# A hybrid decoder layer: an eighth Strassen pair in the up-projection, and the last gate's first half summed beside the out-projection

## The chip, the cores and the metric

The kernel runs on one core of a Trainium2 chip. Time is device microseconds of one launch, taken as the median of several executions. The core has a matrix engine (TensorE, PE in the profile, with its weight loads as PEld), a vector engine (DVE), an activation engine (ACT), a general engine (POOL) and a queue processor (SP). SP, ACT and POOL issue DMAs; each engine works through its own instructions in order.

## The reference

One layer for 512 tokens of width 1024. The condition `c` gives six rows of 1024 (shift, scale and gate of the two halves of the layer). The part that matters here is the second half, and the row `gt2`:

```python
mod = silu(c) @ w_ada + b_ada
sh1, sc1, gt1, sh2, sc2, gt2 = split(mod, 6)
...
x = x + gt1 * (concat(o_hg, o_nsa) @ w_out)
h2 = rmsnorm(x, norm2_g) * (1.0 + sc2) + sh2
u = causal_dwconv(h2 @ w_up, conv_w, conv_b)      # w_up: 1024 x 5632, width-3 convolution over tokens
a, v = split(u, 2)
x = x + gt2 * ((silu(a) * v) @ w_down)            # w_down: 2816 x 1024
```

All of it is float32. Every operand of a large matmul is held as two parts, high and low, and a product is three matmuls (high by high, high by low, low by high).

## The kernel before

**Order.** The instructions are issued in the order of the program, engine by engine; nothing reorders them. Tiles come from pools. The pool of granules (`G`, 33 of 4 KB in each partition) holds the long-lived parts; `TMP` gives temporaries, `PS` one of eight banks of PSUM.

**Tiles of the up-projection.** `up_mm(st)` makes tile `st` of 44: 128 rows of u by 512 tokens, 8 blocks of K by three matmuls, 24 matmuls of 512 columns. Tile `st` belongs to f = st // 2 (22 pairs of rows of a and v); even `st` is a, odd `st` is v. `up_post(st)` does the convolution (an activation on ACT, L1633, and two operations on DVE, L1634 and L1635), silu for a (L1638), and for v the product of the two (L1641); then `g_parts` queues the splits that the down-projection needs, and `step(n)` does n of these.

**Units.** Of four tiles, a unit makes the first two together by Strassen's scheme: seven products (P1 to P7) of half of K by half of the tokens, 12 matmuls of 256 columns each, in place of 48 of 512. The other two (B and C) are full tiles. The units are j = `NB` to `NU`; the string `UNIT` is their order, with a prime on a token that prepares the next unit. `PRO` is the order of the prologue that comes ahead: M1 to M7 are tiles 1 to 7 of the matmuls, q0 to q6 `up_post`, F and A the weight forms of a tile (`piece`), t the sums of h2 that the products need, x `step(1)`, n1', f2' and so on the forms of the first unit, m0' the weight forms of its first full tile. In an F form ACT makes the high part and DVE the low part; in an A form the low part is a negated copy by ACT to which POOL adds the source by an adding DMA (L260). After the units come plain tiles; `PLAIN` has a word for each, an A for an A form, and the number of gate steps.

**The gate.** `ada_last` makes `gt2` in two halves of 512 columns. Each half is zeroed, its first partition gets the bias, and eight blocks of rows of `w_ada` (256 KB each) are loaded, multiplied by a column of silu(c) and added, by DVE. The sum is split, and two matmuls with a matrix of ones (L1426, L1427) sum over the partitions and spread the row to all of them; ACT copies it back. It is a generator: the token g takes one step of it. Before, there are 20 steps: three g in `PRO`, one in each of the seven units, ten in the plain tiles, and all its loads are on SP's queue.

**The out-projection** runs ahead of that, tokens in four tiles: `hg_mix` and `hg_flip` make the left operand, `out_mm` the product, `out_sum` adds gate and residual, `out_norm` takes the norm, where `rstd` ends with a power on POOL (L393), `out_scale` and `h2_flip` turn the result.

**Parking.** The parts of a pair j of the down-projection are two granules, gP and gQ. For j in `AWAY`, gQ goes to memory (`park`, on ACT's queue) and comes back in the down-projection's first phase (`load_away`, called by `each_a` at every second step from the fourth on, on SP's queue).

Of the kernel before, what the change touches and what calls it, by code (L numbers as in the profile page):

```python
# [10 lines left out]
F32 = mybir.dt.float32  # L11
# [5 lines left out]
ALU = mybir.AluOpType  # L17
# [3 lines left out]
P = 128  # L21
# [17 lines left out]
SCRATCH = 1024  # L39
LAG = 4  # L40
NB = 2
NU = 8
AWAY = (0, 1)
CUT = {"B": 6, "C": 7}
ADD = (1, 1)
PLAIN = "2 A1 1 1 A2 1 1 1"
PRO = ("t t g x M1 M2 t t t t F3 M3 F4 t A5 q0 M4 q1 q2 F6 q3 M5 M6 A7 x q4 g x q5 x t x n1' ns' f2' nc' n5' q6 na' g s4' m0' x x M7 m1' x f6' f7' x x x x f4'")
UNIT = ("P1 S P5 w n1' ns' x f3 B0 P6 P2 B1 V x f2' nc' n5' h1 x p-1 f4' P7 x m0' P3 h0' W p2 g p0 na' C0 P4 x x x C1 s4' p1 x m1' x f6' x x x f7'")
PREP = ('sq2 sq3 rq2 rq3', '', 'nq0', 'fq0', 'nq1', '', 'lq0', 'fq1', 'nq2', '', 'lq1', 'fq2', 'nq3', 'lq2', 'fq3',
        'lq3', 'sk0 rk0 sk1 rk1', 'nk0 fk0 sk2 rk2', 'nk1 fk1 sk3 rk3', 'lk0 nk2 fk2', 'lk1 nk3 fk3 sa0 ra0',  # L50
# [61 lines left out]
def hybrid_layer_kernel(ctx: ExitStack, tc: tile.TileContext, d: dict, out: bass.AP, dbg=None):  # L112
# [24 lines left out]
    def TMP(shape, dt=F32, tag="tmp"):  # L137
        n = 1
        for a in shape[1:]:
            n *= a  # L140
        if n > 256:
            return tp.tile(shape, dt, tag="t2", name=nm(tag), bufs=9)
        return tp.tile(shape, dt, tag="t1", name=nm(tag), bufs=4)
# [4 lines left out]
    def f32(ap):  # L148
        return ap.bitcast(F32)

    def split(hi, lo, src, eng=None):
        sc.copy(hi, src)  # L152
        (eng or ve).tensor_tensor(lo, src, f32(hi), ALU.subtract)  # L153
# [236 lines left out]
    def rstd(o, s, scale, eps):  # L390
        n = s.shape[-1]
        ve.tensor_scalar(o, s, scale, eps, ALU.mult, ALU.add)  # L392
        gp.tensor_tensor(o, o, mhalf[:, 0:n], ALU.pow)  # L393
# [881 lines left out]
    ons = {}  # L1275
    mixH = [None] * NT

    def hg_mix(i):
        ps = PS("hgo")
        for h in range(4):  # L1280
            AD, QP, S = As[h // 2]
            j = h % 2
            pe.matmul(ps[:, h * P:(h + 1) * P], AD[:, j, i], HV[j][:, i, h // 2 * P:h // 2 * P + P], start=True,
                      stop=(i == 0))
            if i:
                pe.matmul(ps[:, h * P:(h + 1) * P], QP[:, j, i * P:(i + 1) * P], S[:, j, i - 1], start=False, stop=True)
        sq = TMP([P, 512], tag="sqh")
        sc.activation(sq, ps, AF.Square)
        s = SM([P, 8], "hss")
        ve.tensor_reduce(s[:, 0:4], sq.rearrange("p (h e) -> p h e", h=4), AX.X, ALU.add)  # L1290
        r = SM([P, 8], "hrs")
        rstd(r[:, 0:4], s[:, 0:4], 1.0 / P, 4.0 * EPS)
        on = TMP([P, 4, P], tag="on")
        ve.tensor_tensor(on, ps.rearrange("p (h e) -> p h e", h=4),
                         r[:, 0:4].unsqueeze(2).to_broadcast([P, 4, P]), ALU.mult)
        ons[i] = on

    def hg_flip(i):
        on = ons.pop(i)
        ps = PS()  # L1300
        for h in range(4):
            pe.transpose(ps[:, h * P:(h + 1) * P], on[:, h], ident)
        m = G([2, 4, P], F32R, s="mixH")
        t = TMP([P, 4, P], tag="og")
        for pr in range(2):
            ve.scalar_tensor_tensor(t[:, 2 * pr:2 * pr + 2], ps[:, pr * 256:pr * 256 + 256]
                                    .rearrange("p (h t) -> p h t", h=2), hgg,
                                    HGT[pr][:, :, i * P:(i + 1) * P], ALU.mult, ALU.mult)
        split(m[:, 0], m[:, 1], t)
        mixH[i] = m  # L1310


# [86 lines left out]
    def ada_last(s, res):  # L1399
        for q in range(2):  # L1400
            acc = res[:, q * 512:(q + 1) * 512]
            c0 = s * D + q * 512
            gp.memset(acc, 0.0)
            sp.dma_start(acc[0:1], d["b_ada"][:, c0:c0 + 512])
            for k in range(KT if q else 0):
                raw = TMP([P, 512], tag="ada2r")
                sp.dma_start(raw, ada_view[:, k, c0:c0 + 512])
                if k:
                    yield
                    ve.scalar_tensor_tensor(acc, last, cs[:, k - 1:k], acc, ALU.mult, ALU.add)  # L1410
                last = raw
            for k in range(0 if q else KT):
                last = res[:, 512:]
                if k:
                    ve.scalar_tensor_tensor(acc, last, cs[:, k - 1:k], acc, ALU.mult, ALU.add)
                sp.dma_start(last, ada_view[:, k, c0:c0 + 512])
                if k < KT - 1:
                    yield
            yield
            ve.scalar_tensor_tensor(acc, last, cs[:, k:k + 1], acc, ALU.mult, ALU.add)  # L1420
            hi = TMP([P, 512], F32R, tag="rhi")
            lo = TMP([P, 512], F32R, tag="rlo")
            split(hi, lo, acc)
            yield
            ps = PS()
            pe.matmul(ps, onesr, hi, start=True, stop=False)  # L1426
            pe.matmul(ps, onesr, lo, start=False, stop=True)  # L1427
            sc.copy(acc, ps)
            yield


    x1 = []
# [144 lines left out]
    for i in range(NT):  # L1577
        x1.append(G([D], s="x1"))
        sp.dma_start(x1[i], x_view[:, i])
    next(gate1)  # L1580
    hg_mix(0)
    next(gate1)
# [1 line left out]
    out_mm(0, 0, KN)  # L1584
    cols_sum(acol)
    hg_flip(0)
    hg_mix(2)
    hg_mix(3)
    out_mm(1, 0, KN)
    for _ in gate1:  # L1590
# [1 line left out]
    out_weights("oh", 0, 0)  # L1592
    out_mm(2, 0, KN)
    hg_flip(1)
    hg_flip(2)
    out_mm(3, 0, KN)
    out_mm(0, 0, KH)
    hg_flip(3)
# [146 lines left out]
    def do_(j, tok):  # L1745
        lo_, hi_ = lo_half, hi_half
        w = forms7.get(j)
        u = partial(u_of, j)
        if tok == "P1":
            banks(j)  # L1750
            sprod(u(1, lo_), w[1], h2_quarter(0, lo_), True)
        elif tok == "P5":
            sprod(us["x", j][:, lo_], w[5], h2_summed(1), True)
        elif tok == "P6":
            sprod(u(1, lo_), w[6], h2_summed(2))
        elif tok == "P2":
            sprod(u(0, lo_), w[2], h2_quarter(1, lo_))
        elif tok == "P7":
            sprod(u(1, lo_), w[7], h2_summed(3))
        elif tok == "P3":  # L1760
            sprod(u(0, hi_), w[3], h2_quarter(1, hi_))
        elif tok == "P4":
            sprod(u(1, lo_), w[4], h2_summed(4))
        elif tok in ("B0", "B1", "C0", "C1"):
            up_mm(4 * j + (2 if tok[0] == "B" else 3), full, (range(0, CUT[tok[0]]), range(CUT[tok[0]], KT))[int(tok[1])])
        elif tok == "S":
            sc.copy(u(0, lo_), u(1, lo_))
        elif tok == "w":
            spare(j)
        elif tok == "V":  # L1770
            ve.tensor_tensor(u(0, hi_), u(1, lo_), ws5[j], ALU.add)
        elif tok == "W":
            ve.tensor_tensor(u(1, hi_), u(1, lo_), ws5[j], ALU.add)
        elif tok[0] == "p":
            up_post(4 * j + int(tok[1:]))
        elif tok == "x":
            step(1)
        elif tok == "g":
            next(ada2, None)
        elif tok == "t":  # L1780
            turn()
        elif tok[0] == "m":
            std_make(j, int(tok[1]))
        elif tok[0] == "h":
            h = high.pop(4 * j + 2 + int(tok[1]))
            if h:
                h()
        elif tok == "n1":
            pair_open(j)
        elif tok == "ns":  # L1790
            pair_sum(j)
        elif tok == "nc":
            pair_less(j, 2, 0, 2)
        elif tok == "na":
            pair_less(j, 0, 4, 0)
        elif tok == "s4":
            pair_less(j, 1, 1, 0)
        elif tok == "n5":
            split(*w[5], quads[j][4])
        else:  # L1800
            pair_form(j, int(tok[1]), {6: 0, 2: 1, 7: 2, 3: 1, 4: 3}[int(tok[1])])
# [139 lines left out]
        ve.tensor_tensor(t, t, rest[i][:, cols], ALU.add)  # L1941
        sp.dma_start(out_view[:, i, cols], t)

    gt2 = wp.tile([P, D], F32, tag="xin", name="gt2", bufs=1)
    ada2 = ada_last(5, gt2)
    lo_half, hi_half, full = slice(0, 256), slice(256, 512), slice(0, 512)
    nst = 2 * NFF
    for i in range(NT):
        out_mm(i, 1, KN + KH)
        if i == 0:  # L1950
            conv_weights()
        if i:
            h2_flip(i - 1)
            wts[i - 1] = next_parts(False)
        out_sum(i, 1)
        sc.dma_start(x1d[:, i], x1[i])
        out_norm(i)
        if i:
            h2_scale(i - 1, 0)
            h2_scale(i - 1, 1)  # L1960
        out_scale(i)
        if i:
            h2_split(i - 1)
# [29 lines left out]
    for st in range(first, nst):  # L1993
        up_mm(st, full)
        if st >= nst - 2:
            look()
        if st == first:
            up_post(st - 1)
        elif st > first + 1:
            up_post(st - 2)  # L2000
        for _ in range(int(PLAIN.split()[st - first][-1])):
            next(ada2, None)

    look()
    up_post(nst - 2, False)
    bR, bW, bS, bV = ([PS("dn") for _ in range(2)] for _ in range(4))
# [101 lines left out]
```

## Time and profile before

| | us |
|---|---|
| median of 3 runs | 674.73 (674.34 to 675.54) |
| the profiled execution | 674.35 |
| its span, from the first to the last instruction | 672.6 |
| out-projection and its head, about | 267 to 326 |
| prologue of the up-projection | 326.9 to 372.3 |
| seven units | 372.3 to 520.2 |
| eight plain tiles | 520.2 to 564.2 |
| down-projection, first to last matmul | 564.2 to 669.1 |

A row of a timeline has start, length, engine, line of the program, operation, output <- inputs, shape and count; in brackets stands how long the engine was idle before it, and what ended that. A row of a group has the count, the busy time and the mean.

### The profile page before, as it was taken

To read this page: it belongs to the slowest core of one execution; us is meant where nothing else is said; L and a number is where in the kernel's file an instruction comes from. 1 tells how busy PE (TensorE), PEld (TensorE's weight loads), DVE (VectorE), ACT (ScalarE), POOL (GpSimd) and SP (SyncE) were. 2 spreads that over 40 slices of the span, in tenths; PEclk is the share of its full clock that TensorE was granted. 3 is DMA by queue.
4 is the path that set the end of the run, shared out by engine and by line. 5 is a ranking of instruction groups with operands and counts; after the bars stand their busy time and mean duration, and the time that the engine had idled before them with its cause. 6 is when DMAs were issued, how large, how long until landed. Compare 5 with 4: busy or idle time off the path is not lost.

```text
span 672.6 us, 10869 instructions
## 1 busy us (share of the span) xinstructions
PE 664.9 (99%) x3999; PEld 565.1 (84%) x3999; DVE 577.8 (86%) x1155; ACT 392.6 (58%) x757; POOL 60.0 (9%) x80
## 2 busy tenths in 40 slices
PE   8999999999999999999999999999999999999998
PEld 4678898788898889888998888989888888888886
DVE  5688988999998997687878988998898789988787
ACT  5564446666677688335665766667675455553431
POOL 1006144200000000200000011010110000000000
PEclk9999999999999999999999999999999999999999
DMA  9998444388042132435436677986779773979932
GB/s 279 287 322 269 145 157 138 106 288 254 11 147 95 33 107 99 172 96 161 140 95 172 179 196 198 242 218 175 187 181 277 217 234 124 393 259 398 388 112 94
DMA packets 110473, 128.52 MB, mean 191 GB/s; under 512 B 7067, under 2 KB 84691, under 8 KB 110421
## 3 DMA queue, kind: packets, MB, share of 16 engines
q1 hardware_dynamic: 103541, 106.89, 51.1%
q0 software_dynamic: 2448, 8.91, 6.9%
q10 hardware_dynamic: 4432, 12.04, 4.7%
q8 instruction: 31, 0.51, 0.3%
q14 instruction: 21, 0.17, 0.1%
HBM read 105.01 MB, written 13.90 MB: 177 GB/s over the span
## 4 chain that ended last, share of the span: by engine, by line
PE 92%; SPq 3%; DMA 2%; DVE 1%; issue 0%; ACTq 0%; ACT 0%
PE u L156 11%; PE u L158 11%; PE u L157 11%; PE dn L157 5%; PE dn L156 5%; PE dn L158 5%; PE pT L156 3%; PE pT L158 3%; PE pT L157 3%; PE F L1059 3%; PE oT L1087 3%; PE oh L158 2%; PE oh L156 2%; PE oh L157 2%; SPq L317 2%; PE lev L1188 2%
## 5 line engine op out<-in xcount | busy, mean ns | idle before, releaser
L156 PE MATMUL u<-h2h,whi 128*128 128x512 f32 (+1 forms) x208 | 78.0, 375 | 0.0
L157 PE MATMUL u<-h2l,whi 128*128 128x512 f32 (+1 forms) x208 | 77.8, 374 | 0.0
L158 PE MATMUL u<-h2h,wlo 128*128 128x512 f32 (+1 forms) x208 | 77.6, 373 | 0.0
L153 DVE TENSOR_TENSOR wlo<-raw,whi 128x1024 fp32r<-128x1024 f32 (+1 forms) x38 | 44.5, 1170 | 6.7 <-ACT whi L152 6.5
L152 ACT CAST whi<-raw 128x1024 fp32r<-128x1024 f32 (+1 forms) x38 | 38.3, 1008 | 18.8 <-PE u L157 7.3
L158 PEld LDWEIGHTS u<-h2h,wlo 128*128 128x128 f32 x208 | 39.2, 188 | 7.5 <-DVE wlo L153 0.4
L156 PEld LDWEIGHTS u<-h2h,whi 128*128 128x128 f32 x208 | 39.3, 189 | 6.0
L157 PEld LDWEIGHTS u<-h2l,whi 128*128 128x128 f32 x208 | 39.3, 189 | 5.8
L1027 ACT ACTIVATE pt<-pt,mx 128x128 f32<-128x128 f32 (+3 forms) x64 | 35.9, 562 | 11.8 <-DVE mx L1011 10.7
L1634 DVE SCALAR_TENSOR_TENSOR y<-u,cv,y 128x511 f32<-128x511 f32 x44 | 32.8, 745 | 11.4 <-ACT y L1633 11.4
L156 PE MATMUL pT<-hT,whi 128*128 128x512 f32 x96 | 39.2, 408 | 0.0
L1638 ACT ACTIVATE y<-y 128x512 f32<-128x512 f32 x21 | 13.3, 633 | 42.0 <-DVE y L1635 42.0
L158 PE MATMUL pT<-hT,wlo 128*128 128x512 f32 x96 | 37.7, 393 | 0.0
L157 PE MATMUL pT<-hT,whi 128*128 128x512 f32 x96 | 37.6, 391 | 0.0
L1011 DVE CUSTOM_DVE_ANT_0 pt<-S,cmask 128x128 f32<-128x128 f32 (+3 forms) x64 | 29.7, 484 | 6.5 <-PE S L1006 6.3
L1066 ACT COPY pT<-F 128x512 f32<-128x512 f32 (+2 forms) x52 | 25.9, 503 | 14.4 <-PE F L1059 11.2
L1635 DVE SCALAR_TENSOR_TENSOR y<-u,cv,y 128x510 f32<-128x510 f32 x44 | 32.9, 749 | 1.6
L1633 ACT ACTIVATE y<-u,cv 128x512 f32<-128x512 f32 x44 | 33.8, 771 | 0.0
L393 POOL TENSOR_TENSOR hrs<-hrs,mhalf 128x4 f32<-128x4 f32 (+2 forms) x16 | 20.0, 1259 | 136.4 <-DVE hrs L392 136.3
L157 PE MATMUL u<-h2l,w 128*128 128x256 f32 (+1 forms) x84 | 28.0, 333 | 0.0
L156 PE MATMUL u<-h2h,w 128*128 128x256 f32 (+1 forms) x84 | 28.0, 333 | 0.0
L158 PE MATMUL u<-h2h,w 128*128 128x256 f32 (+1 forms) x84 | 28.0, 333 | 0.0
(456 smaller groups left out, 2079.2 us busy)
## 6 DMA issues: line engine op xcount, KB each, us to landing
raw<-in_w_up SPq DMA_DIRECT2D x44, 512.0 KB, 5.6
aw<-in_w_ada SPq DMA_DIRECT2D x24, 512.0 KB, 3.6
raw<-in_w_down SPq DMA_DIRECT2D x10, 1024.0 KB
ada<-in_w_ada SPq DMA_DIRECT2D x32, 256.0 KB, 5.8
wlo<-raw POOLq DMA_DIRECT2D x15, 512.0 KB, 4.6
raw<-in_w_in SPq DMA_DIRECT2D x7, 1024.0 KB, 6.1
rawd<-in_w_down SPq DMA_DIRECT2D x12, 512.0 KB, 10.3
pk<-st ACTq DMA_DIRECT2D x11, 512.0 KB, 4.0
```

Of the source, the lines that this page charges most:

```text
L152: sc.copy(hi, src)
L153: (eng or ve).tensor_tensor(lo, src, f32(hi), ALU.subtract)
L156: pe.matmul(o, ah, bh, start=start, stop=False, skip_group_check=True)
L157: pe.matmul(o, ah, bl, start=False, stop=False, skip_group_check=True)
L158: pe.matmul(o, al, bh, start=False, stop=stop, skip_group_check=True)
L1011: ve.tensor_tensor_reduce(pt[:, sl], ps[:, sl], cmask[:, 512 - W:512], -1.0, 1e30, ALU.add, ALU.min, mx[:, e:e + 1])
L1027: sc.activation(pt[:, sl], pt[:, sl], AF.Exp, bias=mx[:, e:e + 1], scale=-1.0, accum_out=su[:, h % 2, e:e + 1])
L1059: pe.transpose(ps[:, j * P:(j + 1) * P], src[:, j * P:(j + 1) * P], ident)
L1066: sc.copy(pT, ps[:, 0:n * P])
L1633: sc.activation(y, u, AF.Identity, bias=cv[:, 132 + c:133 + c], scale=cv[:, 88 + c:89 + c])
L1634: ve.scalar_tensor_tensor(y[:, 1:], u[:, :T - 1], cv[:, 44 + c:45 + c], y[:, 1:], ALU.mult, ALU.add)
L1635: ve.scalar_tensor_tensor(y[:, 2:], u[:, :T - 2], cv[:, c:c + 1], y[:, 2:], ALU.mult, ALU.add)
```

## The change

`NU` goes from 8 to 9, so that the units are j = 2 to 9 and four plain tiles are left. `AWAY` goes from two granules to four. `ada_last` is cut into steps half as long (its load and its sum are separate steps, 40 in all), it takes its loads for the first half on POOL's queue and for the second on SP's, and each half has one buffer for its loads (the second half a stretch of the constants that is no longer read). It is made ahead of the out-projection: a first pair of steps there, one step within `hg_mix(2)` and one behind it, the same at `hg_flip(2)`, two in each of the four tiles of tokens around `out_norm`. Three g of two steps are in `PRO`, one in each unit, and one in each of the first two plain tiles.

```diff
-NU = 8
-AWAY = (0, 1)
+NU = 9
+AWAY = (0, 1, 2, 3)
-PLAIN = "2 A1 1 1 A2 1 1 1"
-PRO = ("t t g x M1 M2 t t t t F3 M3 F4 t A5 q0 M4 q1 q2 F6 q3 M5 M6 A7 x q4 g x q5 x t x n1' ns' f2' nc' n5' q6 na' g s4' m0' x x M7 m1' x f6' f7' x x x x f4'")
+PLAIN = "1 A1 0 A0"
+PRO = ("t t x M1 M2 t t t t F3 M3 F4 t A5 g q0 M4 g q1 q2 g F6 q3 M5 M6 A7 x q4 x q5 x t x n1' ns' f2' nc' n5' q6 na' s4' m0' x x M7 m1' x f6' f7' x x x x f4'")
...
-    def hg_mix(i):
+    def hg_mix(i, between=lambda: None):
...
         rstd(r[:, 0:4], s[:, 0:4], 1.0 / P, 4.0 * EPS)
+        between()
         on = TMP([P, 4, P], tag="on")
...
-    def hg_flip(i):
+    def hg_flip(i, between=lambda: None):
...
-        split(m[:, 0], m[:, 1], t)
+        sc.copy(m[:, 0], t)
+        between()
+        ve.tensor_tensor(m[:, 1], t, f32(m[:, 0]), ALU.subtract)
...
     def ada_last(s, res):
         for q in range(2):
             acc = res[:, q * 512:(q + 1) * 512]
+            last = cb[:, C_LMASK:C_LMASK + 512] if q else res[:, 512:]
             c0 = s * D + q * 512
             gp.memset(acc, 0.0)
-            sp.dma_start(acc[0:1], d["b_ada"][:, c0:c0 + 512])
...
+            gp.dma_start(acc[0:1], d["b_ada"][:, c0:c0 + 512])
+            for k in range(KT):
                 if k:
                     ve.scalar_tensor_tensor(acc, last, cs[:, k - 1:k], acc, ALU.mult, ALU.add)
...
+                yield
+                (sp if q else gp).dma_start(last, ada_view[:, k, c0:c0 + 512])
+                yield
             ve.scalar_tensor_tensor(acc, last, cs[:, k:k + 1], acc, ALU.mult, ALU.add)
             hi = TMP([P, 512], F32R, tag="rhi")
             lo = TMP([P, 512], F32R, tag="rlo")
             split(hi, lo, acc)
             yield
+            yield
             ps = PS()
             pe.matmul(ps, onesr, hi, start=True, stop=False)
             pe.matmul(ps, onesr, lo, start=False, stop=True)
             sc.copy(acc, ps)
             yield
+            yield
+
+    def gate_step(n=2):
+        for _ in range(n):
+            next(ada2, None)
...
+    gt2 = wp.tile([P, D], F32, tag="xin", name="gt2", bufs=1)
+    ada2 = ada_last(5, gt2)
+    gate_step()
     next(gate1)
...
-    hg_mix(2)
+    hg_mix(2, partial(gate_step, 1))
+    gate_step(1)
...
-    hg_flip(2)
+    hg_flip(2, partial(gate_step, 1))
+    gate_step(1)
...
         elif tok == "g":
-            next(ada2, None)
+            gate_step()
...
         sc.dma_start(x1d[:, i], x1[i])
+        gate_step(1)
         out_norm(i)
+        gate_step(1)
...
         for _ in range(int(PLAIN.split()[st - first][-1])):
-            next(ada2, None)
...
+            gate_step()
```

More of the change, by code (lines that the diff above doesn't have):

```diff
@@ L1401, in ada_last @@
             acc = res[:, q * 512:(q + 1) * 512]
+            last = cb[:, C_LMASK:C_LMASK + 512] if q else res[:, 512:]
             c0 = s * D + q * 512
             gp.memset(acc, 0.0)
-            sp.dma_start(acc[0:1], d["b_ada"][:, c0:c0 + 512])
[L1405 to L1413, printed above, removed]
+            gp.dma_start(acc[0:1], d["b_ada"][:, c0:c0 + 512])
+            for k in range(KT):
                 if k:
                     ve.scalar_tensor_tensor(acc, last, cs[:, k - 1:k], acc, ALU.mult, ALU.add)
[L1416 to L1419, printed above, removed]
+                yield
+                (sp if q else gp).dma_start(last, ada_view[:, k, c0:c0 + 512])
+                yield
             ve.scalar_tensor_tensor(acc, last, cs[:, k:k + 1], acc, ALU.mult, ALU.add)
@@ L1942, in dn_out @@
         sp.dma_start(out_view[:, i, cols], t)
-    gt2 = wp.tile([P, D], F32, tag="xin", name="gt2", bufs=1)
-    ada2 = ada_last(5, gt2)
     lo_half, hi_half, full = slice(0, 256), slice(256, 512), slice(0, 512)
@@ L2001, in hybrid_layer_kernel @@
         for _ in range(int(PLAIN.split()[st - first][-1])):
-            next(ada2, None)
+            gate_step()
+    assert next(ada2, 0) == 0
     look()
```

## The prediction, made before the changed kernel was run

> **What bounds the kernel now.** I read the page first: its span and its busy shares.
>
> ```profile
> span 672.6 us, 10869 instructions
> ...
> PE 664.9 (99%) x3999; PEld 565.1 (84%) x3999; DVE 577.8 (86%) x1155; ACT 392.6 (58%) x757; POOL 60.0 (9%) x80
> ```
>
> TensorE is busy for 664.9 of 672.6 us, so time can only come from fewer or shorter matmuls, or from new waits of TensorE. The table of who waited shows no idle TensorE after the first 100 us. A busy PE is modelled, though, so I read the spacing of matmul starts in the timeline of PE, over the whole up-projection.
>
> ```profile
> 361.44 0.39 PE L156 MATMUL u<-h2h,w 128*128 128x512 f32 x1
> ...
> 366.88 0.39 PE L156 MATMUL u<-h2h,whi 128*128 128x512 f32 x1
> ...
> 375.19 0.40 PE L156 MATMUL u<-h2h,whi 128*128 128x512 f32 x1
> 375.42 0.40 PE L157 MATMUL u<-h2l,whi 128*128 128x512 f32 x1
> 375.82 0.50 PE L158 MATMUL u<-h2h,wlo 128*128 128x512 f32 x1
> ...
> 414.64 0.28 PE L156 MATMUL u<-h2h,w 128*128 128x256 f32 x1
> ...
> 435.67 0.28 PE L156 MATMUL u<-h2h,w 128*128 128x256 f32 x1
> ```
>
> The first two rows open the tiles M6 and M7 of the prologue: a full tile (24 matmuls) takes 366.88 - 361.44 = 5.44 us. The last two open the product P1 of two successive units: a unit (seven half-size products and two full tiles) takes 435.67 - 414.64 = 21.03 us. The three rows in the middle are the one place where TensorE stumbles: they begin B0, the first full tile of the first unit, and its third matmul, the first to read wlo, comes 0.40 us after the second where others come 0.23 us apart. That wlo is made by DVE. So at B0 the chain of DVE and ACT through the prologue has no slack at all: what makes that chain later makes TensorE later by the same. The rows of that chain, from the timelines of DVE and of ACT (the number in brackets is the engine's idle time before the row, and what ended it):
>
> ```profile
> 315.78 0.16 DVE L1515 TENSOR_TENSOR ss<-ss 128x1 f32<-128x1 f32 x1 [0.79 <-ACT sq L1512]
> ...
> 348.00 0.75 DVE L1634 SCALAR_TENSOR_TENSOR y<-u,cv,y 128x511 f32<-128x511 f32 x1 [0.92 <-ACT y L1633]
> 348.78 0.75 DVE L1635 SCALAR_TENSOR_TENSOR y<-u,cv,y 128x510 f32<-128x510 f32 x1
> 352.23 0.75 DVE L1634 SCALAR_TENSOR_TENSOR y<-u,cv,y 128x511 f32<-128x511 f32 x1 [2.70 <-ACT y L1633]
> ...
> 357.64 1.23 DVE L153 TENSOR_TENSOR w<-raw,w 128x1024 fp32r<-128x1024 f32 x1 [1.70 <-ACT w L152]
> ...
> 374.55 1.22 DVE L153 TENSOR_TENSOR wlo<-raw,whi 128x1024 fp32r<-128x1024 f32 x1
> ```
>
> ```profile
> 350.90 0.63 ACT L1638 ACTIVATE y<-y 128x512 f32<-128x512 f32 x1
> 351.44 1.43 ACT L1633 ACTIVATE y<-u,cv 128x512 f32<-128x512 f32 x2
> 356.03 0.63 ACT L1638 ACTIVATE y<-y 128x512 f32<-128x512 f32 x1 [3.16 <-DVE y L1635]
> 356.57 1.04 ACT L152 CAST w<-raw 128x1024 fp32r<-128x1024 f32 x1
> ...
> 367.08 0.62 ACT L152 CAST w<-raw 128x512 fp32r<-128x512 f32 x1 [1.93 <-PE u L158]
> ```
>
> In tokens of PRO: 348.00 and 348.78 are q0; 351.44 on ACT opens q1 and q2; 352.23 is q1 on DVE; the silu of q2 at 356.03 is followed by F6 on ACT (356.57) and on DVE (357.64), which M6 needs; 374.55 is m0', which B0 needs. The two engines hand this chain back and forth in program order, so a delay put in at q1 arrives whole at m0'.
>
> **The change part by part.** *One more unit.* Four full tiles, 4 x 5.44 = 21.76 us, become one unit, 21.03 us: 0.73 us less. The eighth unit's forms, like those of the other seven, are made in the unit before it, and no unit after the first shows a spacing that is not matmul alone; I take the same for the new one.
>
> *The gate's matmuls.* The broadcast of each half of the gate is two 128x512 matmuls.
>
> ```profile
> L1426 PE MATMUL ps<-rhi,onesr x2: 389/392/396, 512.9 to 563.8; 128*128 128x512 f32 x2
> ```
>
> One of the pairs moves from unit 8 (512.9) to the prologue, between M4 and M5, the other to an earlier plain tile. At 0.227 us (5.44 / 24) each, 0.45 us leaves unit 8 and comes into the prologue: no change in sum.
>
> *The gate's sums beside the out-projection.* Seven sums of the first half go on DVE there, each after its load. One sum costs what it does now.
>
> ```profile
> L1415 DVE SCALAR_TENSOR_TENSOR gt<-gt,cs x7: 742/745/746, 362.7 to 474.4; 128x512 f32<-128x512 f32 x7
> ```
>
> The change puts each into a gap where DVE waits for another engine; for the row at 315.78 the gap is 0.79 us against 0.745 us. I take nothing for them. Their loads are issued by POOL, behind rstd's power in its queue, and each has until the next tile of tokens to land. If that cover goes, the cost is DVE time ahead of out_scale; TensorE waits only for what exceeds the slack there, and I leave up to 0.5 us for it in the range.
>
> *The gate's last load and its end, in the prologue.* Here I expect the price. The new PRO has three g, of two steps each: the first adds row block 6 and issues the load of block 7 on POOL; the second adds block 7 and splits the sum (ACT, then DVE); the third is the pair of matmuls and ACT's copy. The first stands behind A5, whose low part is an adding DMA in the same POOL queue; only q0 and M4 stand between the first and the second. Rows: POOL's timeline; then the transfer of A5, from issue to landing; then windows (length, busy time of PE, PEld, DVE, ACT and POOL, clock, DMA share, GB/s).
>
> ```profile
> 310.93 0.55 POOL L393 TENSOR_TENSOR rs<-rs,mhalf 128x1 f32<-128x1 f32 x1 [24.84 <-DVE rs L392]
> ...
> 346.69 1.08 POOL L260 DMA_DIRECT2D wlo<-raw  x1 [15.45 <-ACT wlo L259]
> ```
>
> ```profile
> DMA to landing us min/median/max: 6.2/6.2/6.2
> ```
>
> ```profile
> 349.40:352.50 3.10, 3.10 (x15) 2.57 (x14) 0.40 (x2) 2.88 (x4) 0.00 (x0) 1.00 0.98 199
> 352.50:354.00 1.50, 1.50 (x9) 1.23 (x8) 1.43 (x3) 0.37 (x1) 0.00 (x0) 1.00 0.00 0
> ```
>
> A5's DMA is issued at 346.69 and lands at 352.9; the DMA engines are full (0.98) up to 352.5 and then idle. The first sum fits into the 0.92 us gap before 348.00, so POOL can issue the load of block 7 at about 347.9, behind A5's transfer in the same queue. No trace shows two transfers of POOL in flight together. From below: it runs as if alone. A load of a block by SP, 256 KB, took
>
> ```profile
> DMA to landing us min/median/max: 2.8/2.8/2.8
> ```
>
> at 374.05, and POOL's issue takes 1.08 us in the row above where SP's takes about half a us less: 347.9 + 2.8 + 0.6 = 351.3. From above: it begins only when A5 has landed, 352.9 + 2.8 = 355.7. I take the DMA engines' own end, 352.5, plus 256 KB at the 199 GB/s of that window (1.3 us), 353.8, as nearest to what the windows show.
>
> DVE has q0 done at 349.5 and then stands at the second g, with q1 and q2 queued behind it; ACT stands at the split's first half, with the activations of q1 and q2 behind it. Before, q1's activation began at 351.44. After: 353.8 + 0.745 (sum) + 0.62 (cast of 128x512, as at 367.08) = 355.2, 3.7 us later. Between the silu of q2 and F6 ACT also gets the copy of the third g, for which I put 0.5 us, an estimate from the same 0.62 us less the overlap of neighbours. F6's low part then ends near 363.1 in place of 358.9, M6 waits some 0.5 us for it, and the chain goes on 4.2 us late. Two sums of the old prologue (362.7, 373.3) leave DVE, but behind each the next step waits for ACT, so I credit 0.1 us. At B0 the lag is 4.1 us, and TensorE, with nothing to spare there, takes all of it. What TensorE did in that time is 0.45 us of moved matmuls.
>
> [...]
>
> *The second half.* Its bias and memset go to POOL in the first unit, and its eight loads to SP's queue, one in each unit behind a sum of 0.745 us, as the first half's loads stood there before; the old plain tiles had two or three. Behind each such load stand the up-projection's loads, as now. I take nothing.
>
> *Four parked granules.* Two more stores and two more reloads of 512 KB; the reloads join SP's queue in the first phase of the down-projection.
>
> ```profile
> 586.00:596.00 10.00, 10.00 (x46) 8.28 (x45) 7.67 (x9) 7.29 (x11) 0.00 (x0) 1.00 0.86 340
> ```
>
> The row is ahead of the first use of the reloaded granules (phase 1, about 599). The 1 MB is 3.1 us of transfer at 340 GB/s, and a seventh of the window (1.4 us) is free; the rest pushes loads that are themselves early. I take nothing, and up to 1 us if it isn't so.
>
> **The sum.** -0.73 (unit) + 4.1 (lag at B0) - 0.45 (matmuls that left unit 8) = +2.9 us, against the profiled execution's 674.35 us (its span, 672.6 us, and 1.75 us around it): 677.2 us. The median shown is 674.73, 0.4 us above that execution. 0.2% of it is 1.35 us, about what a measurement of this kernel can tell from no change.
>
> **The rivals.**
> *The load is early.* Block 7 lands at 351.3, not queued behind A5. q1's activation begins at 352.7, 1.3 us late, the copy adds 0.5: 1.8 - 1.18 = +0.6 us, 675.0. Against it: the full DMA engines up to 352.5.
> *All hidden: faster.* The stall never reaches TensorE, because the removed sums and the freed out-projection give the chain slack that I don't see; then -0.73, and B0's 0.17 us of today go too: 673.45, the fast end. It decides if block 7 lands before 349.6, when DVE reaches it. More than 1.35 us can be won only if the plain tiles' lighter DVE and ACT load also shortens the down-projection, where I find no wait to remove: about 672.8.
> *The load is late and more waits.* It begins after A5 has landed (355.7): 1.9 us more, 679.1; with late gate loads in the out-projection (0.5) or the reloads (1.0) to 680.6.
> *The unit does not do what it says:* if the new unit ran short of granules it would last as long as four tiles, +0.7 us on any case above: 677.9 on mine.
>
> **How the numbers follow.** My forecast, with the last rival within it, 0.62; late 0.12; early 0.15 (most of it within 0.2%); all hidden 0.11 (0.04 within 0.2%, 0.07 past it). Slower by over 0.2%: 0.62 + 0.12 and a little of early: 0.76. Same: 0.17. Faster: 0.07. The forecast's own range is 676.0 to 678.3. To hold 8 in 10 I go down to 674.4, which takes in the early case, and up to 679.2, which takes in the late load; left out are all hidden and the sums of several mishaps.
>
> **What would show it.** Right: unit starts still 21.03 us apart, and one more of them; a gap of about 4 us on DVE ended by a DMA of the gate between q0 and q1; ACT's activation of q1 near 355; B0 some 4 us later after M4 than before; no new idle time in the out-projection. Wrong: if block 7's sum starts before 351, the lag is not there; if B0 is late but the gap isn't, something else in the prologue, such as banks or temporaries, holds it; if the time comes in the down-projection, it is the reloads.

## The result and the profile after

| us | before | after |
|---|---|---|
| median, six runs each | 675.13 (673.99 to 676.29) | 681.0 (679.8 to 681.44) |
| profiled execution | 674.35 | 679.8 |
| its span | 672.6 | 678.0 |

The ratio is 1.0085, with a 95% interval of 1.0071 to 1.0100: the change makes the kernel slower, by 5.45 us between the profiled executions and 5.9 us between the medians. The page of the changed kernel begins with its span and the busy shares.

```profile
span 678.0 us, 10958 instructions
...
PE 667.0 (98%) x4035; PEld 565.9 (83%) x4035; DVE 581.4 (86%) x1165; ACT 395.7 (58%) x765; POOL 67.4 (10%) x91
```

TensorE has been given about 2 us of apparent work and 5.4 us of span: it waits. Where, the timeline of PE says, as in the prediction by starts of matmuls (start, length, engine, line, operation, output <- inputs; in brackets the wait and what ended it). Lines of the changed kernel lie six further down: L1633 is now L1639.

```profile
373.62 0.28 PE L156 MATMUL u<-h2h,w 128*128 128x256 f32 x1
...
378.57 0.50 PE L156 MATMUL u<-h2h,whi 128*128 128x512 f32 x1 [1.64 <-ACT whi L152]
378.92 0.39 PE L157 MATMUL u<-h2l,whi 128*128 128x512 f32 x1
379.83 0.50 PE L158 MATMUL u<-h2h,wlo 128*128 128x512 f32 x1 [0.53 <-DVE wlo L153]
...
397.69 0.28 PE L156 MATMUL u<-h2h,w 128*128 128x256 f32 x1
...
418.71 0.28 PE L156 MATMUL u<-h2h,w 128*128 128x256 f32 x1
...
440.14 0.28 PE L156 MATMUL u<-h2h,w 128*128 128x256 f32 x1
...
446.89 0.39 PE L158 MATMUL u<-h2h,wlo 128*128 128x512 f32 x1
447.73 0.39 PE L156 MATMUL u<-hS,wq 128*128 128x256 f32 x1 [0.46 <-ACT u L1773]
...
462.10 0.28 PE L156 MATMUL u<-h2h,w 128*128 128x256 f32 x1
...
484.00 0.28 PE L156 MATMUL u<-h2h,w 128*128 128x256 f32 x1
...
505.03 0.28 PE L156 MATMUL u<-h2h,w 128*128 128x256 f32 x1
```

The rows with `h2h,w` and 256 columns open P1 of units 2 to 8. B0 of unit 2 now waits for both its parts, whi and wlo, and its third matmul starts at 379.83 where it started at 375.82. That is the place the prediction named. The periods then are 24.07 us (unit 2), 21.02 (unit 3), and **21.43, 21.96 and 21.90 for units 4 to 6** before 21.03 returns: 2.2 us that the prediction does not have. In each of these three units TensorE stands where the row 447.73 stands, at P6, behind the copy of P1 by ACT (token S); in unit 4 it is P6's weight load that waits, 0.29 us. In unit 5 the copy begins 5.13 us behind P1 before the change and 7.18 us after it. Over the runs below a unit loses what its copy begins later than some 6.25 us behind P1: nothing at 6.19 (e3, unit 5), 0.16 us at 6.46 (e8, unit 4), 0.51 at 6.72 (e4, unit 5), 0.93 at 7.18 here. So unit 5 had some 1.1 us to spare at S before the change. Unit 2's chain begins where it was expected. The timelines of DVE, then of ACT:

```profile
347.28 0.74 DVE L1411 SCALAR_TENSOR_TENSOR gt<-gt,cs 128x512 f32<-128x512 f32 x1
...
349.07 0.75 DVE L1641 SCALAR_TENSOR_TENSOR y<-u,cv,y 128x510 f32<-128x510 f32 x1
353.73 0.75 DVE L1415 SCALAR_TENSOR_TENSOR gt<-gt,cs 128x512 f32<-128x512 f32 x1 [3.91 <-DMA gt<-in_w_ada]
...
361.73 1.23 DVE L153 TENSOR_TENSOR w<-raw,w 128x1024 fp32r<-128x1024 f32 x1 [2.18 <-ACT w L152]
```

```profile
355.05 1.44 ACT L1639 ACTIVATE y<-u,cv 128x512 f32<-128x512 f32 x2
...
360.19 0.57 ACT L1424 COPY gt<-ps 128x512 f32<-128x512 f32 x1
...
457.06 1.06 ACT L1700 ACTIVATE wlo<-raw 128x1024 fp32r<-128x1024 f32 x1 [2.48 <-DMA raw<-in_w_up]
```

DVE is idle for 3.91 us between q0 and q1, ended by the gate's load; q1's activation begins at 355.05 (355.2 was forecast), F6's low part at 361.73 ends at 362.96 (363.1 was forecast). The last row stands in unit 5: it is the step whose lateness e4 looks into.

Put together, against the kernel before: the first matmul of the up-projection is 0.3 us later in this execution (327.16 against 326.87; among the runs below it lies anywhere from 326.33 to 327.35, so this is scatter of the start); P1 of unit 2 is 1.0 us later than that, by the moved matmuls (0.45) and M6's wait; unit 2 lasts 2.8 us longer; units 4 to 6 2.2 us longer; the ninth unit saves 0.73 and the matmul pair that left unit 8 0.45. The sum is 5.1 us, and the last matmul is 5.1 us later (674.19 against 669.08). The down-projection lasts as long as before.

### The profile page after: what moved, and what is told of

Its sections match the earlier page's. It is cut to its first block, busy times and chain, and to the rows that moved or that the text cites. A ratio compares the mean times of both kernels' runs of the same rounds, so it can differ in the third digit from the quotient of the medians.

```text
span 678.0 us, 10958 instructions
## 1 busy us (share of the span) xinstructions
PE 667.0 (98%) x4035; PEld 565.9 (83%) x4035; DVE 581.4 (86%) x1165; ACT 395.7 (58%) x765; POOL 67.4 (10%) x91
## 4 chain that ended last, share of the span: by engine, by line
PE 76%; DVE 7%; DMA 6%; ACT 6%; SPq 3%; issue 2%; ACTq 0%; DVEq 0%
PE u L158 6%; PE u L156 6%; PE u L157 6%; PE dn L157 5%; PE dn L158 5%; PE dn L156 5%; PE pT L156 3%; PE pT L158 3%; PE pT L157 3%; PE F L1059 3%; PE oT L1087 3%; DMA raw<-in_w_up 2%; SPq L317 2%; PE oh L158 2%; PE oh L156 2%; PE oh L157 2%
## 5 line engine op out<-in xcount | busy, mean ns | idle before, releaser
L156 PE MATMUL u<-h2h,whi 128*128 128x512 f32 (+1 forms) x200 | 75.1, 375 | 1.6 <-ACT whi L152 1.6
L158 PE MATMUL u<-h2h,wlo 128*128 128x512 f32 (+1 forms) x200 | 74.6, 373 | 0.5 <-DVE wlo L153 0.5
L157 PE MATMUL u<-h2l,whi 128*128 128x512 f32 (+1 forms) x200 | 74.8, 374 | 0.0
L153 DVE TENSOR_TENSOR wlo<-raw,whi 128x1024 fp32r<-128x1024 f32 (+1 forms) x35 | 40.8, 1166 | 6.8 <-ACT whi L152 6.6
L158 PEld LDWEIGHTS u<-h2h,wlo 128*128 128x128 f32 x200 | 37.7, 188 | 8.1 <-DVE wlo L153 1.0
L156 PEld LDWEIGHTS u<-h2h,whi 128*128 128x128 f32 x200 | 37.8, 189 | 7.3 <-ACT whi L152 1.8
L152 ACT CAST whi<-raw 128x1024 fp32r<-128x1024 f32 (+1 forms) x35 | 35.1, 1004 | 13.6 <-PE kva L158 4.4
L1639 ACT ACTIVATE y<-u,cv 128x512 f32<-128x512 f32 x44 | 33.8, 770 | 0.0
L152 ACT CAST wq<-raw 128x512 fp32r<-128x512 f32 x40 | 24.6, 617 | 11.6 <-DVE w L153 7.2
L153 DVE TENSOR_TENSOR wq<-raw,wq 128x512 fp32r<-128x512 f32 x40 | 27.3, 684 | 1.6 <-ACT wq L152 1.6
L156 PE MATMUL u<-hS,wq 128*128 128x256 f32 x96 | 27.5, 287 | 0.7 <-ACT u L1773 0.7
```

Of the source, the lines that this page charges most:

```text
L156: pe.matmul(o, ah, bh, start=start, stop=False, skip_group_check=True)
L157: pe.matmul(o, ah, bl, start=False, stop=False, skip_group_check=True)
L158: pe.matmul(o, al, bh, start=False, stop=stop, skip_group_check=True)
L1639: sc.activation(y, u, AF.Identity, bias=cv[:, 132 + c:133 + c], scale=cv[:, 88 + c:89 + c])
```

## The experiments

Each row gives the whole time and two sums read from that run's matmul starts. "Head" is the time from the first matmul of the up-projection to P1 of unit 3, less that of the kernel before (66.74 us): what prologue and first unit lose; those of e3, e10 and e11 hold a slow stretch of 1.6 us that is told of at the end. "Units" is how much the periods of units 3 to 8 (7 in the run of e4) exceed 21.03. The kernel before was run again beside each set; its medians lie between 674.46 and 675.13, and each ratio is against its own set.

| run | median | ratio to before, 95% | head | units |
|---|---|---|---|---|
| changed kernel | 681.0 | 1.0085 (1.0071 to 1.0100) | 3.8 | 2.2 |
| e1 PRO's g at the old places | 677.41 | 1.0040 (1.0028 to 1.0052) | 1.3 | 2.3 |
| e2 block 7's load early | 677.17 | 1.0034 (1.0022 to 1.0046) | 0.95 | 2.4 |
| e3 AWAY 0, 1, 4, 5 | 680.42 | 1.0080 (1.0064 to 1.0096) | 5.2 | 2.1, moved |
| e4 before, four parks | 676.83 | 1.0030 (1.0020 to 1.0040) | 0.0 | 1.55 |
| e5 = e2, gQ stored later | 674.3 | 0.9994 (0.9985 to 1.0003) | 0.95 | 0 |
| e6 = e2, gQ stored by POOL | 678.57 | 1.0056 (1.0043 to 1.0069) | 0.95 | 4.1 |
| e7 = e2, gate loads on POOL | 677.43 | 1.0038 (1.0025 to 1.0050) | 0.95 | 2.8 |
| e8 = e2, two parks | 677.72 | 1.0043 (1.0030 to 1.0055) | 0.95 | 1.4 |
| e9 = e5, gate's end in the units | 675.3 | 1.0015 (1.0006 to 1.0024) | -0.05 | 0.45 |
| e10 = changed, gQ stored later | 679.38 | 1.0065 (1.0053 to 1.0078) | 5.4 | 0 |
| e11 = changed, block 7 by SP | 680.77 | 1.0087 (1.0074 to 1.0101) | 5.4 | 2.4 |
| e12 = e9, last steps earlier | 679.85 | 1.0076 (1.0062 to 1.0091) | -0.05 | 0.45 |

Two theories were to be told apart for units 4 to 6: that the parks cost this by themselves, or that a prologue which hands over late leaves the units without slack. The rival within the first was what of a park costs: ACT's time to issue it, its traffic, or SP's order.

**e1: undo the move of the gate's steps in PRO.**

```diff
-... t A5 g q0 M4 g q1 q2 g F6 q3 ... q4 x q5 ... na' s4' m0' ...
+t t g x M1 ... t A5 q0 M4 q1 q2 F6 q3 ... q4 g x q5 ... na' g s4' m0' ...
```

> Changed kernel with the three g of PRO back at the places that they had before the change (one at its head, one behind q4, one ahead of s4'), all else as changed. Block 7's load is then issued at about 329, long ahead of A5, and nothing of the gate stands between q0 and F6. Theory 'prologue lag': the 4.0 us at B0 go, up to the 0.45 us of the gate's matmuls that come back into the first unit. Units 4 to 6, which lost 2.2 us, tell two theories apart: if they lose because of the added parks or gate loads (their own cost), they still lose about 2 us and the profiled time is near 676; if they lose because the prologue left DVE and ACT late, they lose nothing and the time is near 673.7, below the kernel before.

The head shrinks from 3.8 to 1.3 us, so the place of the g is the price there. Up to 0.45 us was expected to stay, for the pair of matmuls ahead of unit 2; the other 0.84 us are in unit 2, where wlo still comes late at B0 (TensorE waits 0.53 us for it); their cause stays open. Units 4 to 6 lose 2.3 us as in the changed kernel: their loss is not left over from the prologue. The second theory falls.

**e2: only the load of block 7 earlier.** The sum, the split and the matmuls stay between q0 and F6.

```diff
-t t x M1 ... t A5 g q0 M4 g q1 q2 g F6 ...
+t t g x M1 ... t A5 q0 M4 g q1 q2 g F6 ...
```

> Changed kernel with only the first of PRO's three g at its old place at the head: block 7's load is issued at about 329, ahead of A5; its sum, split and matmuls stay between q0 and F6. My reading of the 4 us is: 2.2 to 3 us of them the wait for the load behind A5's adding DMA, the rest the sum, the cast and the copy themselves. Then q1's activation begins near 352.7 in place of 355.05, B0's lag shrinks from 4.0 to about 1.7 us, and the profiled time is 2.3 us below that of the changed kernel, near 677.5. If the load's place doesn't matter (rival: the split and the copy are what holds the chain), the time stays near 679.8.

Rows of this run, of POOL, DVE and ACT, and what the transfer took from issue to landing:

```profile
339.63 0.54 POOL L1413 DMA_DIRECT2D gt<-in_w_ada  x1 [8.73 <-DVE gt L1411]
```

```profile
349.01 0.74 DVE L1415 SCALAR_TENSOR_TENSOR gt<-gt,cs 128x512 f32<-128x512 f32 x1
```

```profile
351.52 1.44 ACT L1639 ACTIVATE y<-u,cv 128x512 f32<-128x512 f32 x2
```

```profile
gt<-in_w_ada POOLq DMA_DIRECT2D x1, 256.0 KB, 3.0
```

The load goes out at 339.63, later than the 329 I expected since its sum stands behind other work on DVE, and lands 3.0 us later. Block 7's sum follows q0 with no idle time, and q1's activation begins at 351.52 (this run is 0.44 us early at the first matmul, so 0.5 us later than before). I had expected 352.7. Of the head's 3.8 us the wait for the load is 2.8; the matmuls, the split and the copy are 0.95, half of it the matmuls.

**e3 and e4: other granules, and the parks alone.**

```diff
-AWAY = (0, 1, 2, 3)
+AWAY = (0, 1, 4, 5)
```

The second of these edits is on the kernel before:

```diff
-AWAY = (0, 1)
+AWAY = (0, 1, 2, 3)
```

> Changed kernel with the parks of pairs 4 and 5 in place of 2 and 3: the same number of stores, the third and fourth gQ stores fall some two units later. Theory 'parks': the lengthened periods (21.43, 21.96, 21.90 for units 4 to 6) move two units later, to units 6 to 8, and units 4 and 5 come back to 21.03; total about as the changed kernel, 679.8. Rival 'lag': units 4 to 6 stay as they are whatever is parked there, for their lateness comes from the prologue and the sum in each unit. Rival 'granules': if gQ of 2 and 3 must be free by then, waits show elsewhere and the time is longer.

> Kernel before with AWAY of four granules and nothing else changed: the parks alone. By my prediction this costs nothing: 674.4. Theory 'parks by themselves': units 4 to 6 lose up to 2.2 us, 676.5. Theory 'parks only on top of a late chain': below 0.5 us here, 674.9 at most.

In e3 units 7 and 8 last 22.01 and 21.78 us and units 5 and 6 21.03: the loss goes with the store, to the unit after the one in which it is issued. Unit 4 keeps its 0.33 us, and the total loss is 2.1. In e4, the kernel before with nothing but two more parks, units 5 and 6 lose 0.51 and 1.04 us. Its P1 rows:

```profile
436.06 0.28 PE L156 MATMUL u<-h2h,w 128*128 128x256 f32 x1
...
457.60 0.28 PE L156 MATMUL u<-h2h,w 128*128 128x256 f32 x1
...
479.67 0.28 PE L156 MATMUL u<-h2h,w 128*128 128x256 f32 x1
...
500.70 0.28 PE L156 MATMUL u<-h2h,w 128*128 128x256 f32 x1
```

So parks cost by themselves, 2.1 us in the medians, and "up to 2.2 us" was the nearest of the expectations. What is late is ACT's first step on the weights of the next unit's full tiles (m0', the ADD form). The half of the load that it reads is the first one that SP issues in the unit, ahead of the gate's load. Its issue and ACT's step in unit 4, in which the first additional store is issued (421.94), of before and then of e4:

```profile
424.30 0.37 SPq L223 DMA_DIRECT2D raw<-in_w_up  x1
...
428.57 1.06 ACT L1694 ACTIVATE wlo<-raw 128x1024 fp32r<-128x1024 f32 x1 [2.12 <-DMA raw<-in_w_up]
```

```profile
425.32 0.37 SPq L223 DMA_DIRECT2D raw<-in_w_up  x1
...
430.56 1.06 ACT L1694 ACTIVATE wlo<-raw 128x1024 fp32r<-128x1024 f32 x1 [2.50 <-DMA raw<-in_w_up]
```

Counted from P1 (414.64 and 415.03) the step starts at 13.9 and 15.5 us; in both ACT has been idle for over 2 us and the load ended that. Of the 1.6 us the load's issue accounts for 0.6 (9.7 us behind P1, then 10.3) and its travel for 1.0 (4.27 us from issue to ACT's step, then 5.24). In unit 5, behind the second additional store, the step starts at 16.7 us in place of 13.9. Windows of unit 4 show what the load meets, for before and for e4 (the last two columns are DMA share and GB/s):

```profile
425.00:430.00 5.00, 5.00 (x35) 4.62 (x34) 4.93 (x10) 2.88 (x5) 0.00 (x0) 1.00 0.75 220
```

```profile
425.00:430.00 5.00, 5.00 (x35) 4.61 (x34) 4.93 (x10) 3.05 (x5) 0.00 (x0) 1.00 0.99 296
```

In the 5 us in which the up loads travel a quarter of the DMA engines was free; in e4 they are full (0.99), and the load lands later. Its issue waits for a buffer that DVE frees in the same unit (in the kernel before SP stands 14.9 us for DVE's `wq` ahead of the issue at 424.30), so a late ACT and DVE make the load late as well. p2's activation is queued behind m0' on ACT and DVE behind that, so the next unit's S comes late: this is how the lateness passes from unit to unit. The 1.6 us of unit 4 are there again at unit 5's S, which begins 6.72 us behind P1 in place of 5.13; less the 1.1 us to spare they make the 0.51 us that unit 5 loses.

**e5, e6, e7: when, by whom, and in whose order.** All three start from e2. e5 keeps the store on ACT and moves it to the token g; e6 keeps its place and gives it to POOL; e7 leaves the stores and takes the gate's loads off SP. Their edits, in this order:

```diff
     def park(j, st22, st34):
         if j in AWAY:
-            sc.dma_start(pk26[:, AWAY.index(j)], f32(gQ.pop(j)))
+            later.append((pk26[:, AWAY.index(j)], f32(gQ.pop(j))))
...
         elif tok == "g":
             gate_step()
+            if later:
+                sc.dma_start(*later.pop(0))
```

```diff
-            sc.dma_start(pk26[:, AWAY.index(j)], f32(gQ.pop(j)))
+            gp.dma_start(pk26[:, AWAY.index(j)], f32(gQ.pop(j)))
```

```diff
-                (sp if q else gp).dma_start(last, ada_view[:, k, c0:c0 + 512])
+                gp.dma_start(last, ada_view[:, k, c0:c0 + 512])
```

> The kernel of e2 with each of the four gQ stores issued later, at the token g of the same unit (some 17 us into the unit in place of 8), by the same engine, with the same bytes; the two other stores of park stay where they are. In the run of e4 the second up load of a unit lands about 2.5 us later where a gQ store stands ahead of it, about what 512 KB takes. Theory 'traffic': the store takes the DMA engines from the up loads; issued after they have landed it costs nothing, units 4 to 6 come back to 21.03 (from 21.42, 22.00 and 22.03) and the median is about 674.9, 2.3 us below e2. Theory 'issue time': ACT's 0.33 us for each more store is what is late; it stays, and so do some 2 us. Rival: the granule comes free about 9 us later and an allocation waits for it; then new waits and a longer time than e2.

> The kernel of e2 with the four gQ stores issued by POOL at the same step, in place of ACT: ACT's issue time for them is gone, their bytes and about their time are the same. Theory 'traffic': units 4 to 6 lose as in e2, about 2.3 us, median 677. Theory 'issue time': they lose nothing, 674.9. A queue of their own may let them run beside the other stores, or behind A-form transfers of POOL; up to 1 us either way.

> The kernel of e2 with the second half's eight gate loads on POOL's queue in place of SP's, where each stands between the first and the second up load of its unit. Theory 'SP's order': the gate load holds the second up load back (its issue takes SP 1.3 to 2.1 us where gQ is stored, 1.0 before); without it that load is issued some 1 to 2 us earlier, units 4 to 6 lose under 1 us, median about 675.5. Theory 'traffic': the same bytes contend as before, the loss stays near 2.3 us, 677.

e5's P1 rows of units 4 to 6:

```profile
415.68 0.28 PE L156 MATMUL u<-h2h,w 128*128 128x256 f32 x1
...
436.71 0.28 PE L156 MATMUL u<-h2h,w 128*128 128x256 f32 x1
...
457.73 0.28 PE L156 MATMUL u<-h2h,w 128*128 128x256 f32 x1
```

Every unit after the first lasts 21.03 again: the same stores, by the same engine, with the same bytes, cost nothing when they are issued behind the unit's up loads. The median is 674.3, 2.9 us below e2 and within what can be told from the kernel before. In e6, with ACT rid of the issue, the units lose more, not less (4.1 us; the ADD form's first step starts 17.8 us into unit 5). So ACT's issue time is not needed for the loss, and what has to change is the place of the store ahead of the load.

The travel of the load that ACT waits for, from its issue to ACT's step, goes with the store. In units 3 to 7 of the kernel before, the changed kernel and e1 to e6, e8 and e10 it is 4.3 to 4.8 us where no such store goes out ahead of the load in the unit (once 5.1), 5.0 to 6.1 us behind a store by ACT (4.7 in unit 3 of the kernel before, where ACT waited for TensorE), and 5.9 to 6.6 us behind e6's stores by POOL. POOL's store goes out 2.6 us ahead of the load in unit 4 and takes 6.5 us; ACT's goes out 3.4 us ahead of it in e4. So a store by ACT makes the load's travel about 1 us longer, not the 2.5 us that the expectation of e5 speaks of. ACT's longer stand at its park adds to it in e4 (in unit 4 the third issue takes 1.03 us where the last one took 0.33, and the next cast begins 8.9 us behind P1 where it began 7.6 behind it).

e7 shows no gain, 2.8 us against 2.4: SP's order of the gate's loads is not the cause. The load that ACT waits for goes out ahead of the unit's gate load (424.30 and 426.39 in the kernel before), so the gate's load can't hold it back as the expectation has it.

**e8: without the two parks**, from e2.

```diff
-AWAY = (0, 1, 2, 3)
+AWAY = (0, 1)
```

> The kernel of e2 with the two parks of before in place of four: two granules (512 KB each) less come free. If the ninth unit needs them, allocations wait and the time is longer than e2's 677.2, by one to several us at the end of the units or in the plain tiles. If not, the loss of units 5 and 6 goes (2.0 us), the time is near 675.1, and two of the parks were not needed.

```profile
508.44 0.39 PE L156 MATMUL u<-hS,wq 128*128 128x256 f32 x1 [0.95 <-ACT u L1773]
...
531.27 0.39 PE L156 MATMUL u<-hS,wq 128*128 128x256 f32 x1 [1.56 <-ACT u L1773]
```

Units 5 and 6 are back at 21.03, but units 8 and 9, the last two, now stop at the same place for 1.2 and 1.7 us (508.44 comes 1.34 us after the matmul ahead of it, 531.27 1.95). Without the two parks the last units stop, so the parks are needed; that granules are short there fits, but the rows name ACT and not the allocation, so it is not shown. What the parks cost comes from their moment.

**e9 and e12: nothing of the gate's end in the prologue.** Both from e5; the steps that leave PRO go to the units, and later ones to the plain tiles.

```diff
-t t g x M1 ... t A5 q0 M4 g q1 q2 g F6 ...
+t t g x M1 ... t A5 q0 M4 q1 q2 F6 ...
-PLAIN = "1 A1 0 A0"
+PLAIN = "1 A1 1 A1"
```

and e12, in the last unit, from e9:

```diff
+                if tok == "f7'":
+                    gate_step()
-PLAIN = "1 A1 1 A1"
+PLAIN = "1 A1 1 A0"
```

> The kernel of e5 (deferred gQ stores) with the second and third g of PRO taken out: the first half's last sum and split fall to the g of unit 2, its matmuls and copy to that of unit 3, and two steps of the second half move to the plain tiles. Nothing of the gate but one sum is left in the prologue. If the 0.95 us that e2 and e5 still lose ahead of B0 (0.47 at P1, 0.48 at B0) are the moved matmuls and the split and copy on ACT and DVE, they go: P1 comes as in the kernel before, unit 2 lasts 21.3 or less, and all that is left of the change is the unit's 0.73 us: the profiled time is near 673.5, the median near 673.9. Rival: the units have no room for them either (DVE waits 0.77 us in each, ACT 2.1), unit 2 or 3 lengthens by up to 1 us and the time is that of e5.

> The kernel of e9 with one pair of the gate's steps moved from the last plain tile to the end of unit 9, which prepares no unit after it. In e9 the prologue and the units end 0.8 us ahead of the kernel before, counted from the first matmul of the up-projection, and the first phase of the down-projection gives back 1.5 us in two waits, at 571.4 and 577.6, for weight forms that DVE makes after the gate's late steps. If those steps are what delays them, both waits shrink: profiled time 673.6 to 674.3, median 0.3 to 0.8 us under the kernel before. Rival: the waits stay, because any gate step in the plain tiles costs them; then 675.3 as e9.

In e9 the head's last 0.95 us go (-0.05), the only longer unit is unit 3 by the two matmuls that now stand in it, and the up-projection ends 0.78 us earlier than before, counted from its first matmul (563.23 - 326.67 = 236.56 against 237.34): this is the unit's 0.73 us, seen at last. But the down-projection gives back 1.6 us, 1.3 of it in two waits for weight forms of DVE. e12 was meant to take those away and misses badly:

```profile
557.25 0.75 DVE L1415 SCALAR_TENSOR_TENSOR gt<-cb,cs,gt 128x512 f32<-128x512 f32 x1 [4.84 <-DMA cb<-in_w_ada]
```

```profile
558.71 0.50 PE L1422 MATMUL ps<-rhi,onesr 128*128 128x512 f32 x1 [0.92 <-ACT rhi L152]
...
573.26 0.50 PE L157 MATMUL dn<-w,gP 128*128 128x512 f32 x1 [2.15 <-DVE w L153]
```

The gate's sums of successive tiles share one buffer, so a load is issued only behind the sum before it; in the plain tiles it then stands among the down-projection's own transfers (it is issued at 552.44, and an adding DMA issued by POOL at 548.64 lands at 556.65), and DVE waits 4.84 us for it. That looks like the prologue's stall again at another place; no run took it apart. No version tried is measurably faster than the kernel before; e5 is its equal.

**e10 and e11: the two causes on the changed kernel itself.**

The edit of e10 is that of e5; e11 is:

```diff
-                (sp if q else gp).dma_start(last, ada_view[:, k, c0:c0 + 512])
+                (sp if q or k == KT - 1 else gp).dma_start(last, ada_view[:, k, c0:c0 + 512])
```

> The changed kernel with its own PRO, and only the four gQ stores deferred to the token g. Units 4 to 6 come back to 21.03 and the loss at B0 stays: 679.8 - 2.2 = 677.6 us profiled, what my prediction summed (677.2) plus the later start of that run. If the prologue's lag and the parks' loss feed each other, unit 2 alone would still be long and units 3 to 5 not all 21.03; then between 677.6 and 679.

> The changed kernel with one load, the first half's block 7, issued by SP in place of POOL, at the same point of the program. It tells POOL's queue from the DMA engines as what made it land at 353.71, 5.3 us after its issue. 'Queue': it no longer stands behind A5's adding DMA and lands some 2.8 us after its issue (median of such a load in the trace before), near 351; q1's activation begins near 352.7 and B0's loss shrinks by some 2.3 us: 677.5 profiled. 'Engines full': it shares the engines with A5 and with the 1 MB of the up load ahead of it in SP's own queue and lands past 352.5; the gain is under 1.2 us, 678.6 or more. Units 4 to 6 lose 2.2 us either way.

In e10 units 3 to 8 all last 21.03, and the head keeps its loss: the two causes are independent. Its profiled execution, 678.87, is longer than 677.6 because of that slow stretch in unit 2; without its 1.6 us it is 677.3.

In e11 the load is issued by SP at 347.58, and yet:

```profile
353.39 0.75 DVE L1415 SCALAR_TENSOR_TENSOR gt<-gt,cs 128x512 f32<-128x512 f32 x1 [4.05 <-DMA gt<-in_w_ada]
```

Counted from the first matmul of the up-projection, the sum starts 26.7 us in, against 26.6 in the changed kernel. A5's transfer lands at 353.00 in this run. So it is not POOL's queue. Nor does SP's queue explain it: the up load ahead of it in that queue lands at 350.44 (issued at 345.06, 5.4 us). In both runs the load lands only when A5's transfer is done too: at 353.71 behind 353.10 where POOL issues it, and where SP does, its sum starts at 353.39 behind 353.00. "Engines full" was right: the DMA share is 1.00 from 348.4 to 353.7 in the changed kernel.

## Why the prediction was right and wrong

The direction was right, and so was the mechanism in the prologue. The size was short: 677.2 us forecast, 679.8 in the profiled execution.

- *One more unit, -0.73.* Right. e9 shows it as 0.78 us from the first matmul to the end of the up-projection.
- *The load of block 7.* Taken to land at 353.8; the sum starts at 353.73. I worked it out from the end of the DMA engines' full stretch and not from the queue, and e11 shows that this was the right ground. The words "behind A5's transfer in the same queue" were the weaker half of it: in the changed kernel A5 lands at 353.10 and the block at 353.71, so two transfers of POOL were in flight together. e2's load, in a window with DMA share 0.26, took 3.0 us from issue to landing, the one here, with DMA share 1.00 from 348.4 to 353.7, 5.3 us.
- *The lag at B0, 4.1 us.* 4.0 on the clock of the span, 3.7 without the later start. A mechanism right in place and size; the rival "the load is early" was not met by any run: it has the load land at 351.3 and lose 1.8 us ahead of B0, while in e2 it lands at 342.6 and the head loses 0.95 us with the matmuls.
- *The gate's sums beside the out-projection, at nothing.* Five of the seven start ahead of the up-projection's first matmul, the others at 329.20 and 347.28. Nothing is seen of them: up to the first matmul of the up-projection the runs with and without them differ by no more than the runs of one schedule do.
- *The reloads, at nothing.* Right: the down-projection lasts 104.9 us in both (564.21 to 669.08, 569.30 to 674.19).
- *The step that failed.* "*Four parked granules.* Two more stores and two more reloads of 512 KB", which ends "I take nothing, and up to 1 us if it isn't so". That paragraph prices the two reloads and puts the two stores at nothing without a word on where they fall. Behind it stands "no unit after the first shows a spacing that is not matmul alone; I take the same for the new one". The new unit did run so, 21.03 us like the others; but that a unit's matmuls are gapless says that TensorE had no wait in it, not that DVE and ACT had room. The stores fall into units 4 and 5, ahead of the load that ends ACT's wait each time: a store makes that load's travel about 1 us longer (4.27 to 5.24 us in unit 4), ACT's longer stand at the park comes on top, and only some 1.1 us were spare at the next unit's S. They put 1.8 us into units 5 and 6. A row of the trace before could have shown the edge: the wait of `wlo` for `raw<-in_w_up`, 2.12 us in unit 4.
- *Unit 4's part.* 0.4 of the 2.2 us is in unit 4, behind the store of pair 1 in unit 3, which the kernel before has as well and at no cost. It goes with the deferral (e10), stays with PRO undone (e1) and is not in e4. In unit 3 ACT's step begins 14.3 us behind P1 before and 14.6 in e4, but 15.4 in the changed kernel and 15.5 in e1, and the load's travel is 4.7 and 5.0 us, then 5.3 and 5.7. What makes this older store cost more in the changed kernel stays open.
- *Profiled execution and median.* I took them as one but for 0.4 us. After, the profiled execution is the fastest of six by 1.0 us; a likely reason is in the last section.

With the stores deferred and nothing else mended (e10), the trace is the one that was forecast but for the slow stretch: the lag at B0, then units of 21.03 us.

## What to carry to other kernels

When a store or a load is added, price it at the moment of its issue, against the transfer that ends the next wait, and not only at the place where its data come back: here each added store of 512 KB cost 0.5 to 1.0 us ahead of a load and nothing ten microseconds later in the same unit. A unit in which the bound engine shows no gaps may still have little slack in the engines that feed it, here 1.1 us at S; the row to read is the wait of the feeder for its DMA. And an operation placed one step behind the issue of its own load, at a point where the DMA engines were full, stopped its whole engine here for 3.9 us where POOL issued the load (DMA share 1.00), and for 4.1 us where SP did.

## What the runs showed of the hardware

In four profiled executions a slow stretch came behind short waits of TensorE. In the run of e10 TensorE stands 1.64 us and 0.53 us at B0, and then the same matmuls come 0.43 us apart for 3.4 us, and 0.23 apart after that. Rows of its PE, and windows with the granted clock (the column ahead of the DMA share):

```profile
379.57 0.50 PE L158 MATMUL u<-h2h,wlo 128*128 128x512 f32 x1 [0.53 <-DVE wlo L153]
379.90 0.40 PE L156 MATMUL u<-h2h,whi 128*128 128x512 f32 x1
...
380.38 0.63 PE L158 MATMUL u<-h2h,wlo 128*128 128x512 f32 x1
380.81 0.63 PE L156 MATMUL u<-h2h,whi 128*128 128x512 f32 x1
```

```profile
378.30:380.30 2.00, 1.47 (x5) 0.94 (x6) 2.00 (x4) 2.00 (x5) 0.35 (x1) 1.00 0.02 4
380.30:383.80 3.50, 3.50 (x11) 2.68 (x10) 3.47 (x8) 3.50 (x10) 0.52 (x1) 0.51 0.73 163
383.80:390.00 6.20, 6.20 (x43) 5.75 (x42) 3.73 (x8) 4.41 (x8) 0.00 (x0) 1.00 0.93 273
```

Eight matmuls at 0.427 in place of 0.227 us are 1.6 us more. The profiled executions of e3 (granted clock 0.50 from 379.60 to 383.00) and e11 show the same stretch at the same place, and that of e12 has one that begins 1.9 us behind its 2.15 us wait; all four list a mean granted clock of 0.997. That of the changed kernel, with the same waits at B0, has none, so what sets the stretch off is not shown. The changed kernel's mean granted clock is 1.0 there and its time 679.8; its five other runs list 0.997 and 680.81 to 681.44. Half a clock for 3.4 of 678 us makes a mean of 0.997 (an estimate from the window above), so the median of the changed kernel very likely holds this stretch, though no trace of those five runs shows it. That it explains their time is less sure: the six runs of e3 do not sort that way, with 678.86 to 681.81 at a clock of 1.0 and 680.1 and 680.75 at 0.997.
